# Attention sinks as one more score column, and the last query products and a stored group taken back one unit earlier

## The chip, the cores and the metric

The kernel runs on one core of one Trainium2 chip. The core has five engines that work side by side, each through a queue of its own in order: TensorE (PE in the profile, its weight loads PEld), VectorE (DVE), ScalarE (ACT), GpSimd (POOL), and SyncE (SP), which issues most of the transfers (DMA). The metric is the time of one execution on the device in microseconds, the median of several runs; lower is better.

## What is computed

A trunk of two layers with a batch of 1, 1024 positions and 1024 features in float32: an mLSTM mixer, a feed-forward part, a windowed attention mixer, another feed-forward part, with norms between them. The change touches only the attention. There 16 query heads share 4 key/value heads (4 query heads to a group), and every block of 128 queries sees the keys of its own block and of its two neighbours. Each query head has a *sink*, a number that takes part in the softmax as if it were one more key without a value:

```python
m = jnp.maximum(jnp.max(scores, axis=-1), sink_l)
p = jnp.exp(scores - m[..., None])
denom = jnp.sum(p, axis=-1) + jnp.exp(sink_l - m)
out = jnp.einsum('bchgqk,bckhd->bcqhgd', p, v_band)
out = out / denom.transpose(0, 1, 4, 2, 3)[..., None]
```

## The kernel before

The features lie on the partitions and the 1024 positions along the rows, in tiles of 128 x 1024 ("slabs") from one pool of 46. Each float32 product is made of three products of a high and a low part, and an operand is split by ACT (high part) and DVE or POOL (low part: source minus high part; helper `split`, line 203, and `split_scaled`, line 207; for weights line 190).

The attention (`attn`, line 1372) is one loop over 32 *units*, a unit being one group of four heads and one block of 128 queries, group by group: units 0 to 7 are group 0, 24 to 31 are group 3. Step `i` of the loop issues the softmax of unit `i` (`attn_soft`), the transposes of unit `i-2` (`attn_tr`, line 1313) and the products with the values of unit `i-3` (`attn_pv`, line 1328). Between them it places *fill*, products for TensorE that have nothing to do with the unit: until step 20 the query products of groups 1 to 3 (`rope_in`; a rotation on DVE and POOL, lines 1181 to 1191, ends each half, and line 1200 stores it in the DRAM tensor `bounce`), then the output products of groups 0 and 1 (`out_pair`). The numbers in `plan` say up to which step how many of the query pieces are placed.

The softmax of a unit (`head` and `scale`): TensorE makes the scores of a head with the sign turned (line 1284); one DVE instruction adds the mask, writes them to `e` and gives the smallest value, the negated sink included, to `mx` (`smm` in the trace, line 1289); ACT makes the exponential in place and sums it to `dn` (`smd`, line 1293), and makes the exponential of sink minus maximum in `ek` (`sme`, line 1294). For each pair of heads DVE adds `ek` to `dn` (line 1299) and takes the reciprocal (line 1300), and POOL multiplies the pair by it (line 1301). `e` has three buffers.

The outputs of groups 0 and 1 go to DRAM block by block (`ykeep`, line 1342) and come back as slabs: `take_back` issues the loads (line 724) and returns a function that splits them a step later. At step 20 (`NQ`) `load_x` issues 16 loads of the residual (line 242). At steps 6, 14 and 22 `load_q` and `load_k` load the next group's queries and keys (lines 1236, 1244). All these transfers stand in SP's one queue.

The Tile framework decides the order on each engine from the program's order, its priorities and its own estimate of times; the order is then fixed.

Of the kernel before, what the change touches and what calls it, by code (L numbers as in the profile page):

```python
# [11 lines left out]
F32 = mybir.dt.float32  # L12
F32R = mybir.dt.float32r
I32 = mybir.dt.int32
AF = mybir.ActivationFunctionType
ALU = mybir.AluOpType
# [3 lines left out]
P = 128  # L20
# [18 lines left out]
NQ = 20  # L39
# [15 lines left out]
def weave(main, fill=()):  # L55
    n = 0
    for i, m in enumerate(main):
        m()
        while n < len(fill) * (i + 1) // len(main):
            fill[n]()  # L60
            n += 1
# [20 lines left out]
class Trunk:  # L82
# [1185 lines left out]
    def attn_soft(self, g, b, st):  # L1268
        nc = self.nc
        V, A, G, T = nc.vector, nc.scalar, nc.gpsimd, nc.tensor  # L1270
        k0, nk = self.band(b)
        n = nk * P
        m0 = (k0 - (b - 1)) * P

        def head(hd):
            if hd == 0:
                st["e"] = self.t([P, 4, 3 * P], F32, "e", 3)
                st["m"] = [self.t([P, 4], F32, "sm" + x, 3) for x in "mde"]
            e, (mx, dn, ek) = st["e"], st["m"]
            qst, kk = self.qst[g], self.ks[g]  # L1280
            ps = self.bank("sc")
            lq = qst[hd // 2][:, (hd % 2) * S + b * P:(hd % 2) * S + (b + 1) * P]
            for j in range(2):
                T.matmul(  # L1284
                    ps[:, :n], lhsT=lq, rhs=kk[:, j * S + k0 * P:j * S + (k0 + nk) * P],
                    start=j == 0, stop=j == 1,
                )
            c, s = slice(hd, hd + 1), slice(4 * g + hd, 4 * g + hd + 1)
            V.tensor_tensor_reduce(  # L1289
                out=e[:, hd, :n], in0=ps[:, :n], in1=self.mask[:, m0:m0 + n], scale=1.0, scalar=self.nsink[:, s],  # L1290
                op0=ALU.add, op1=ALU.min, accum_out=mx[:, c],
            )
            A.activation(e[:, hd, :n], e[:, hd, :n], AF.Exp, bias=mx[:, c], scale=-1.0, accum_out=dn[:, c])  # L1293
            A.activation(ek[:, c], mx[:, c], AF.Exp, bias=self.sink[:, s])

        def scale(j):
            e, (mx, dn, ek) = st["e"], st["m"]
            d = dn[:, j:j + 2]
            V.tensor_tensor(d, d, ek[:, j:j + 2], op=ALU.add)  # L1299
            V.reciprocal(d, d)  # L1300
            G.tensor_tensor(  # L1301
                e[:, j:j + 2, :n], e[:, j:j + 2, :n], d.unsqueeze(2).broadcast_to([P, 2, n]), op=ALU.mult,
            )

        return [lambda hd=hd: head(hd) for hd in range(4)], [lambda j=j: scale(j) for j in (0, 2)]

    def attn_tr(self, g, b, st):
# [42 lines left out]
    def attn_setup(self):  # L1350
        nc = self.nc
        V, G = nc.vector, nc.gpsimd
        mask = self.mask = self.const.tile([P, 3 * P], F32, name="mask")
        G.memset(mask, 0.0)
        G.affine_select(
            out=mask[:, 0:P], in_=mask[:, 0:P], pattern=[[1, P]], compare_op=ALU.is_ge,
            fill=-NEG, base=0, channel_multiplier=-1,
        )
        G.affine_select(
            out=mask[:, 2 * P:], in_=mask[:, 2 * P:], pattern=[[-1, P]], compare_op=ALU.is_ge,  # L1360
            fill=-NEG, base=0, channel_multiplier=1,
        )
        raw = self.t([P, 16], F32, "sink", 1)
        nc.sync.dma_start(raw, self.h["sink"])
        self.sink, self.nsink = (self.const.tile([P, 16], F32, name=n) for n in ("sink", "nsink"))
        V.tensor_copy(self.sink, raw)
        V.tensor_scalar(self.nsink, raw, -1.0, None, op0=ALU.mult)

    def attn(self):
        nc = self.nc  # L1370

        def tables():
            for half in range(2):
                for tab in (self.cos, self.sin):
                    tb = tab[:, half * HALF:(half + 1) * HALF]
                    (nc.gpsimd if half else nc.vector).tensor_tensor(tb, tb, self.Rv(half), op=ALU.mult)

        with self.phase("a", 6, dict(mm=3, sc=2, tp=2, mx=1)):
            self.qst, self.ks, self.y23 = {}, {}, [[], []]
            weave(self.rope_in(1, -0.125, tables))  # L1380
            weave(self.rope_in(0, None))
            values = self.attn_values()
            values[4:4] = [lambda: self.load_q(0)]
            values[12:12] = [lambda: self.load_k(0)]
            weave(values)
            units = [(g, b) for g in range(4) for b in range(NC)]
            n = len(units)
            st = [{} for _ in units]
            qs = sum((self.rope_in(1 + g, -0.125) for g in range(1, 4)), [])
            y01 = [[], []]  # L1390
            outs = self.out_pair(y01)
            nq = len(qs) // 6
            for f in qs[:nq]:
                f()

            plan = ((0, nq), (4, len(qs) // 3), (11, 2 * len(qs) // 3), (21, len(qs)), (n + 3, len(qs)))
            no = 0
            backs = {}
            for i in range(n + 3):
                so, sc = self.attn_soft(*units[i], st[i]) if i < n else ([], [])  # L1400
                tr = self.attn_tr(*units[i - 2], st[i - 2]) if 2 <= i <= n + 1 else []
                pv = [lambda: self.attn_pv(*units[i - 3], st[i - 3])] if i >= 3 else []
                main = [pv, tr[:1], so[:1], tr[1:2], so[1:2], tr[2:], so[2:3] + sc[:1], so[3:], sc[1:]]
                main = [m for m in main if m]
                if i % NC == 6 and i < n - NC:
                    g = i // NC + 1
                    main[-1] += [lambda: self.load_q(g), lambda: self.load_k(g)]
                for j in range(2):
                    if i == (13, NQ)[j]:
                        backs[j] = self.take_back(self.ykeep[3 + j], y01[j])  # L1410
                    if i == (14, NQ + 1)[j]:
                        backs[j]()
                if i == NQ:
                    self.load_x(self.xkeep)
                (i0, n0), (i1, n1) = [(p, q) for p, q in zip(plan, plan[1:]) if p[0] <= i < q[0]][0]
                k = n0 + (n1 - n0) * (i + 1 - i0) // (i1 - i0)
                fill, nq = qs[nq:k], k
                if i > NQ:
                    k = len(outs) * (i - NQ) // (n + 2 - NQ)
                    fill, no = fill + outs[no:k], k  # L1420
                weave([lambda m=m: [f() for f in m] for m in main], fill)
            self.norm_begin(3, "forms")
            weave(self.out_pair(self.y23, True))
            self.norm_end()
# [98 lines left out]
```

## Time and profile before

| | |
|---|---|
| median of 3 runs | 2302.26 us (2301.77 to 2305.24) |
| the profiled execution, its own time | 2302.37 us |
| its span, first to last instruction | 2300.6 us |
| TensorE busy | 2216.2 us (96%) |
| VectorE busy | 1404.1 us (61%) |
| ScalarE busy | 837.9 us (36%) |
| GpSimd busy | 587.5 us (26%) |
| the attention's loop, units 0 to 31 | about 1285 to 1546 us of the span |

The profiled execution's time is 1.8 us more than its span, and 0.1 us above the median of the runs. "Busy" counts an instruction from start to end, so a stalled instruction is busy too, and TensorE's instructions overlap in its pipeline.

### The profile page before, as it was taken

What the parts mean: (1) busy time and instruction counts of PE and PEld (TensorE: products, weight loads), DVE (VectorE), ACT (ScalarE), POOL (GpSimd) and SP (SyncE); (2) the same over time, 40 slices, a digit from 0 to 9 for tenths busy, and PEclk for the clock granted to TensorE, in tenths of its full rate; (3) what the DMA queues carried; (4) which work ended last, traced back from release to release, by engine and by line L of the source; (5) the groups of instructions that cost most, each with busy time, mean ns of one, the idle gap of its engine ahead of it and who ended that gap; (6) DMA issues with size and microseconds to landing.
All of it is one profiled execution on the core that took longest, in us unless ns stands there. A gap on an engine that the chain in (4) does not pass through costs nothing.

```text
span 2300.6 us, 28252 instructions
## 1 busy us (share of the span) xinstructions
PE 2216.2 (96%) x10713; PEld 1822.1 (79%) x10713; DVE 1404.1 (61%) x2526; ACT 837.9 (36%) x1544; POOL 587.5 (26%) x398
## 2 busy tenths in 40 slices
PE   7899999998999999999999889898999999999998
PEld 4789888776888888878878777686888888888888
DVE  6455675688666666691224689778766666653112
ACT  4434444343222222321222578774422222232121
POOL 2212213311111111321343455550111111133143
PEclk9999999999999999999999999899999999999999
DMA  3111104232222222641322444602222222163112
GB/s 132 42 37 47 65 19 141 80 110 92 81 77 76 79 82 78 215 155 56 101 74 97 125 142 124 210 10 101 92 83 83 83 83 82 67 235 128 58 53 74
DMA packets 73655, 216.75 MB, mean 94 GB/s; under 512 B 8064, under 2 KB 14720, under 8 KB 73520
## 3 DMA queue, kind: packets, MB, share of 16 engines
q1 hardware_dynamic: 61912, 177.07, 23.5%
q10 hardware_dynamic: 11608, 37.89, 4.1%
q8 instruction: 84, 1.38, 0.2%
q14 instruction: 51, 0.42, 0.1%
HBM read 159.15 MB, written 55.77 MB: 93 GB/s over the span
## 4 chain that ended last, share of the span: by engine, by line
PE 43%; DVE 4%; DMA 3%; ACT 2%; POOL 2%; issue 1%; SPq 0%; POOLq 0%; ACTq 0%; DVEq 0%
PE mm L531 18%; PE mm L636 18%; PE mm L230 3%; DMA slab<-bounce 1%; DMA raw<-in_a_in_dram 1%; PE sc L1284 1%; PE mx L1328 1%; PE tp L1313 1%; ACT e L1293 1%; DMA slab<-ykeep 1%; DVE smd L1299 1%; DVE e L1289 1%; POOL slab L1191 0%; DVE t L203 0%; POOL e L1301 0%
## 5 line engine op out<-in xcount | busy, mean ns | idle before, releaser
L190 POOL TENSOR_TENSOR wl<-raw,wh 128x1024 fp32r<-128x1024 f32 (+2 forms) x96 | 228.7, 2386 | 602.6 <-ACT wh L189 379.2
L636 PE MATMUL mm<-hl,wh 128*128 128x512 f32 (+1 forms) x768 | 288.1, 375 | 1.3 <-DVE hl L611 1.3
L636 PE MATMUL mm<-hh,wl 128*128 128x512 f32 (+1 forms) x768 | 287.8, 375 | 0.1
L636 PE MATMUL mm<-hh,wh 128*128 128x512 f32 (+1 forms) x768 | 287.8, 376 | 0.0
L582 POOL TENSOR_TENSOR t<-t,R 128x512 f32<-128x512 f32 x44 | 58.2, 1322 | 595.1 <-ACT t L581 595.1
L663 DVE TENSOR_TENSOR x<-x,mm 128x512 f32<-128x512 f32 x80 | 54.6, 685 | 203.4 <-PE mm L636 203.4
L636 PEld LDWEIGHTS mm<-hl,wh 128*128 128x128 f32 x768 | 144.3, 188 | 30.0 <-DVE hl L611 1.7
L636 PEld LDWEIGHTS mm<-hh,wl 128*128 128x128 f32 x768 | 144.3, 188 | 28.8 <-POOL wl L190 0.5
L636 PEld LDWEIGHTS mm<-hh,wh 128*128 128x128 f32 x768 | 144.3, 188 | 28.2
L230 PE MATMUL mm<-slab,wh 128*128 128x512 f32 x512 | 152.9, 406 | 5.4 <-ACT wh L189 1.9
L581 ACT ACTIVATE t<-t 128x512 f32<-128x512 f32 x44 | 27.8, 632 | 327.5 <-DVE t L580 327.5
L531 PE MATMUL mm<-f12l,wbh 128*128 128x512 f32 x352 | 138.6, 394 | 0.0
L531 PE MATMUL mm<-f12h,wbl 128*128 128x512 f32 x352 | 138.4, 394 | 0.0
L531 PE MATMUL mm<-f12h,wbh 128*128 128x512 f32 x352 | 138.2, 394 | 0.0
L189 ACT ACTIVATE wh<-raw 128x1024 fp32r<-128x1024 f32 (+3 forms) x106 | 102.0, 968 | 68.4 <-DVE hl L611 43.5
L230 PE MATMUL mm<-hnh,wh 128*128 128x512 f32 x416 | 126.0, 402 | 0.9 <-DVE x L663 0.9
L573 DVE TENSOR_TENSOR t<-mm,t 128x512 f32<-128x512 f32 x44 | 30.4, 692 | 155.3 <-PE mm L531 155.3
L230 PE MATMUL mm<-hnh,wl 128*128 128x512 f32 x416 | 123.7, 398 | 0.4 <-POOL wl L190 0.4
L230 PE MATMUL mm<-hnl,wh 128*128 128x512 f32 x416 | 123.2, 397 | 0.0
L531 PE MATMUL mm<-f34h,wd 128*128 128x512 f32 x352 | 117.8, 395 | 0.0
L531 PE MATMUL mm<-f,wah 128*128 128x512 f32 x352 | 111.8, 398 | 5.7 <-DVE x L704 5.7
L230 PEld LDWEIGHTS mm<-slab,wh 128*128 128x128 f32 x512 | 95.3, 192 | 25.2 <-ACT wh L189 2.7
(291 smaller groups left out, 5285.5 us busy)
## 6 DMA issues: line engine op xcount, KB each, us to landing
raw<-in_ffn_in_dram SPq DMA_DIRECT2D x88, 512.0 KB
hkeep<-hs ACTq DMA_DIRECT2D x44, 512.0 KB
hraw<-hkeep SPq DMA_DIRECT2D x44, 512.0 KB
raw<-in_ffn_out_dram SPq DMA_DIRECT2D x32, 512.0 KB
raw<-in_m_in_dram SPq DMA_DIRECT2D x24, 512.0 KB
xkeep<-x ACTq DMA_DIRECT2D x24, 512.0 KB
bounce<-slab SPq DMA_DIRECT2D x40, 256.0 KB
x<-in_x_dram SPq DMA_DIRECT2D x32, 256.0 KB
```

The lines of the kernel that those rows point to most:

```text
L189: nc.scalar.activation(hi[:, c], r[:, c], AF.Copy)
L190: (nc.vector if fast else nc.gpsimd).tensor_tensor(lo[:, c], r[:, c], hi[:, c].bitcast(F32), op=ALU.subtract)
L230: self.nc.tensor.matmul(st["ps"], lhsT=l, rhs=r, start=j == 0, stop=j == len(jobs) - 1)
L531: self.nc.tensor.matmul(ps, lhsT=l, rhs=r, start=start and j == 0, stop=stop and j == len(jobs) - 1, skip_group_check=True,)
L573: V.tensor_tensor(u2, pb, p1, op=ALU.add)
L581: A.activation(g0, g0, AF.Silu)
L582: G.tensor_tensor(g0, g0, R0, op=ALU.mult)
L636: nc.tensor.matmul(po, lhsT=l, rhs=r, start=j == 0, stop=j == len(jobs) - 1)
L663: V.tensor_tensor(x, x, po, op=ALU.add)
L1284: T.matmul(ps[:, :n], lhsT=lq, rhs=kk[:, j * S + k0 * P:j * S + (k0 + nk) * P], start=j == 0, stop=j == 1,)
L1289: V.tensor_tensor_reduce(out=e[:, hd, :n], in0=ps[:, :n], in1=self.mask[:, m0:m0 + n], scale=1.0, scalar=self.nsink[:, s], op0=ALU.add, op ...
L1293: A.activation(e[:, hd, :n], e[:, hd, :n], AF.Exp, bias=mx[:, c], scale=-1.0, accum_out=dn[:, c])
```

## The change

The sink becomes one more column of `e`. At a unit's first head POOL copies the group's four negated sinks into column `n` of the four heads' rows (line 1279 of the changed kernel), and the exponential runs over `n + 1` columns, so that its sum holds the sink's term already. The separate exponential (`ek`, line 1294), DVE's addition (line 1299), the tile `sme` and the copy of the sinks in `attn_setup` go. The rows of `e` grow from 384 to 385 elements; POOL's scaling and the transposes still use `n` columns.

In `attn` the query products are all placed by step 19 instead of step 20, and the second stored group is loaded at step 19 and split at step 20, one step earlier each. `load_x` stays at step 20, and output products still start with step 21.

```diff
         def head(hd):
             if hd == 0:
-                st["e"] = self.t([P, 4, 3 * P], F32, "e", 3)
-                st["m"] = [self.t([P, 4], F32, "sm" + x, 3) for x in "mde"]
-            e, (mx, dn, ek) = st["e"], st["m"]
+                st["e"] = self.t([P, 4, 3 * P + 1], F32, "e", 3)
+                st["m"] = [self.t([P, 4], F32, "sm" + x, 3) for x in "md"]
+                G.tensor_copy(st["e"][:, :, n:n + 1], self.nsink[:, 4 * g:4 * g + 4].unsqueeze(2))
+            e, (mx, dn) = st["e"], st["m"]
...
-            A.activation(e[:, hd, :n], e[:, hd, :n], AF.Exp, bias=mx[:, c], scale=-1.0, accum_out=dn[:, c])
-            A.activation(ek[:, c], mx[:, c], AF.Exp, bias=self.sink[:, s])
+
+            x = e[:, hd, :n + 1]
+            A.activation(x, x, AF.Exp, bias=mx[:, c], scale=-1.0, accum_out=dn[:, c])
...
         def scale(j):
-            e, (mx, dn, ek) = st["e"], st["m"]
+            e, (mx, dn) = st["e"], st["m"]
             d = dn[:, j:j + 2]
-            V.tensor_tensor(d, d, ek[:, j:j + 2], op=ALU.add)
             V.reciprocal(d, d)
...
-        self.sink, self.nsink = (self.const.tile([P, 16], F32, name=n) for n in ("sink", "nsink"))
-        V.tensor_copy(self.sink, raw)
+        self.nsink = self.const.tile([P, 16], F32, name="nsink")
...
-            plan = ((0, nq), (4, len(qs) // 3), (11, 2 * len(qs) // 3), (21, len(qs)), (n + 3, len(qs)))
+            plan = ((0, nq), (4, len(qs) // 3), (11, 2 * len(qs) // 3), (20, len(qs)), (n + 3, len(qs)))
...
-                    if i == (13, NQ)[j]:
+                    if i == (13, NQ - 1)[j]:
                         backs[j] = self.take_back(self.ykeep[3 + j], y01[j])
-                    if i == (14, NQ + 1)[j]:
+                    if i == (14, NQ)[j]:
                         backs[j]()
```

Because the framework orders each queue anew, the change moves more than these lines. Two places are shown. The first is SP's queue around step 20, where `ykeep_67` is the store of group 1, `bounce_120` that of the last group's queries (each row with x2 stands for two stores) and `x_...` are the residual's loads. Before:

```order
L1342 DMA ykeep_67<-R_9190 256x1x128 x4
L1200 DMA bounce_120<-slab_12023 4x32x512
L170 DMA raw_12048<-in_a_out_dram 128x1024
L1200 DMA bounce_120<-slab_12023 4x32x512
L1200 DMA bounce_120<-slab_12024 4x32x512 x2
L724 DMA slab_12145<-ykeep_67 128x1024
L724 DMA slab_12146<-ykeep_67 128x1024
L242 DMA x_12149<-xkeep 128x512
...
L242 DMA x_12156<-xkeep 128x512
L1200 DMA bounce_120<-slab_12260 4x32x512 x2
L1200 DMA bounce_120<-slab_12261 4x32x512 x2
L1236 DMA slab_12456<-bounce_120 128x1024
```

and in the changed kernel:

```order
L1200 DMA bounce_120<-slab_11868 4x32x512 x2
L1200 DMA bounce_120<-slab_11869 4x32x512 x2
L170 DMA raw_11880<-in_a_out_dram 128x1024
L1343 DMA ykeep_67<-R_9188 256x1x128
L724 DMA slab_11954<-ykeep_67 128x1024
L724 DMA slab_11955<-ykeep_67 128x1024
L1200 DMA bounce_120<-slab_12041 4x32x512
L1200 DMA bounce_120<-slab_12042 4x32x512
L242 DMA x_12063<-xkeep 128x512
...
L242 DMA x_12070<-xkeep 128x512
L1236 DMA slab_12316<-bounce_120 128x1024
```

The last four of the eight stores of the last group's queries stood behind the 16 loads of the residual and stand ahead of them now; the loads of the stored group stand right behind the last store of that group and ahead of those four query stores.

The second place is POOL's queue in units 3 to 6. Before, where `e_10642`, `e_10741` and `e_10825` are the tiles of units 3, 4 and 5:

```order
L1301 TENSOR_TENSOR e_10642<-e_10642,smd_10644 128x768
L1190 TENSOR_TENSOR slab_10440<-slab_10440 128x512
L1191 TENSOR_TENSOR slab_10441<-slab_10441 128x512
L1301 TENSOR_TENSOR e_10642<-e_10642,smd_10644 128x768
L1301 TENSOR_TENSOR e_10741<-e_10741,smd_10743 128x768 x2
L1301 TENSOR_TENSOR e_10825<-e_10825,smd_10827 128x768 x2
L190 TENSOR_TENSOR wl_10894<-raw_10409,wh_10893 128x1024
```

and in the changed kernel, where `e_10622`, `e_10715`, `e_10793` and `e_10884` are those of units 3, 4, 5 and 6:

```order
L1302 TENSOR_TENSOR e_10622<-e_10622,smd_10624 128x2x384
L1190 TENSOR_TENSOR slab_10438<-slab_10438 128x512
L1191 TENSOR_TENSOR slab_10439<-slab_10439 128x512
L1302 TENSOR_TENSOR e_10622<-e_10622,smd_10624 128x2x384
L1279 COPY e_10793<-nsink 128x4
L1302 TENSOR_TENSOR e_10715<-e_10715,smd_10717 128x2x384 x2
L1279 COPY e_10884<-nsink 128x4
L1302 TENSOR_TENSOR e_10793<-e_10793,smd_10795 128x2x384 x2
```

The copy for unit 6 stands ahead of the scaling of unit 5; it has to wait until TensorE has transposed unit 3, which used the same buffer.

## Rows read from the trace of the kernel before

**Rows 1.** The page's busy time of each engine: us, share of the span, instructions.

```profile
PE 2216.2 (96%) x10713; PEld 1822.1 (79%) x10713; DVE 1404.1 (61%) x2526; ACT 837.9 (36%) x1544; POOL 587.5 (26%) x398
```

**Rows 2.** Stretches: length, busy PE, PEld, DVE, ACT, POOL, clock, DMA share, GB/s.

```profile
1285.00:1546.20 261.20, 236.56 (x1202) 191.48 (x1203) 220.15 (x585) 194.57 (x548) 145.04 (x105) 0.96 0.37 116
...
1285.60:1322.80 37.20, 31.80 (x156) 25.79 (x154) 31.90 (x79) 24.71 (x73) 19.19 (x14) 0.95 0.19 62
1322.80:1353.40 30.60, 29.87 (x167) 25.06 (x166) 26.23 (x77) 23.73 (x70) 15.24 (x11) 1.00 0.59 161
1353.40:1395.50 42.10, 35.78 (x178) 28.67 (x176) 38.05 (x90) 30.77 (x85) 23.57 (x16) 0.96 0.45 141
...
1431.80:1451.00 19.20, 13.93 (x67) 10.52 (x68) 16.73 (x41) 15.04 (x41) 15.41 (x12) 0.92 0.72 248
...
1465.80:1483.50 17.70, 14.01 (x70) 11.21 (x68) 8.33 (x26) 9.79 (x24) 7.40 (x7) 0.86 0.86 265
...
1479.70:1486.00 6.30, 6.26 (x22) 5.40 (x23) 1.87 (x8) 4.42 (x12) 3.51 (x3) 0.55 1.01 384
```

**Rows 3.** Groups by line and shape, 1285 to 1546: busy us, mean ns, idle before.

```profile
L1301 POOL TENSOR_TENSOR e<-e,smd 128x768 f32<-128x768 f32 x48 | 72.6, 1514 | 61.5 <-DVE smd L1300 48.3 <-ACT sme L1294 8.1 <-ACT t L202 2.2
...
L1293 ACT ACTIVATE e<-e,smm 128x384 f32<-128x384 f32 x96 | 58.5, 609 | 18.3 <-DVE smm L1289 17.2 <-DVE smd L1300 0.6
...
L1294 ACT ACTIVATE sme<-smm,sink 128x1 f32<-128x1 f32 x128 | 36.0, 281 | 0.0
...
L1299 DVE TENSOR_TENSOR smd<-smd,sme 128x2 f32<-128x2 f32 x64 | 29.7, 464 | 5.2 <-ACT sme L1294 5.0
...
L1301 POOL TENSOR_TENSOR e<-e,smd 128x512 f32<-128x512 f32 x16 | 16.6, 1040 | 39.7 <-ACT sme L1294 23.9 <-DVE smd L1300 14.2 <-ACT t L202 0.8
```

**Rows 4.** The chain that ended last, 1284 to 1547: shares; first, last ACT piece.

```profile
by line: PE mm L230 16.1%; DMA slab<-bounce 10.9%; PE sc L1284 7.5%; PE mx L1328 7.4%; PE tp L1313 7.3%; ACT e L1293 6.6%; DMA slab<-ykeep 5.2%; DVE smd L1299 4.9%; issue 4.6%; DVE e L1289 4.4%; DVE t L203 3.6%; POOL e L1301 3.3%; POOL slab
...
1302.82 0.19 ACT sme L1294
...
1527.83 0.19 ACT sme L1294
```

**Rows 5.** Timeline, 1296 to 1306, POOL and DVE: start us, us, instruction.

```profile
1296.88 1.74 POOL L1191 TENSOR_TENSOR slab<-slab 128x512 f32<-128x512 f32 x1
...
1297.39 0.15 DVE L1300 RECIPROCAL smd<-smd 128x2 f32<-128x2 f32 x1
...
1302.90 2.38 POOL L190 TENSOR_TENSOR wl<-raw,wh 128x1024 fp32r<-128x1024 f32 x1 [2.85 <-ACT wh L189]
...
1303.04 2.25 DVE L1299 TENSOR_TENSOR smd<-smd,sme 128x2 f32<-128x2 f32 x1 [0.18 <-ACT sme L1294]
```

**Rows 6.** Tile `smd`: shortest, median, longest ns; first and last start.

```profile
L1299 DVE TENSOR_TENSOR smd<-smd,sme x64: 132/164/2255, 1289.9 to 1534.7; 128x2 f32<-128x2 f32 x64
L1300 DVE RECIPROCAL smd<-smd x64: 145/160/167, 1290.8 to 1534.9; 128x2 f32<-128x2 f32 x64
```

**Rows 7.** SP's issues, timeline 1405 to 1490: start us, us, transfer.

```profile
1431.62 3.69 SPq L724 DMA_DIRECT2D slab<-ykeep  x2
1435.36 16.84 SPq L242 DMA_DIRECT2D x<-xkeep  x16
1452.58 3.83 SPq L1200 DMA_DIRECT2D bounce<-slab  x4
1467.40 2.27 SPq L1236 DMA_DIRECT2D slab<-bounce  x4
```

**Rows 8.** Timeline of PE: idle time before in brackets, and what ended it.

```profile
1448.25 1.65 PE L230 MATMUL mm<-slab,wh 128*128 128x512 f32 x3 [1.64 <-ACT slab L202]
...
1479.74 0.80 PE L1284 MATMUL sc<-slab,slab 128*128 128x256 f32 x2 [3.65 <-DMA slab<-bounce]
```

**Rows 9.** POOL by line and shape, whole span: the smallest instruction.

```profile
L1510 POOL MEMSET const-float32-1.0<- 128x1 f32 x1 | 0.1, 99 | 0.0
```

**Rows 10.** Who waited, 1285 to 1546: us in total, times, longest.

```profile
PE tp L1313 <- POOL e L1301: 3.1, 5, 1.5
```

## The prediction

> **What bounds the kernel now.** I read the page's busy times first [rows 1]: TensorE is busy for 96% of the span, so the rest of the kernel offers nothing to a change on other engines. The change lies in the attention's loop, so I read that stretch next. From 1285 to 1546.2 us TensorE has 236.6 us of busy time in 261.2, at a mean clock of 0.96 [rows 2]. Busy time hides what is lost, because overlapping or slowed matmuls count as busy; a better measure is how many matmuls pass. In the undisturbed stretch 1322.8 to 1353.4 there were 167 in 30.6 us, 0.183 us each, at full clock [rows 2]. At that rate the loop's 1202 matmuls would take 220 us, so about 41 us are lost to waits and low clock. The mix differs a little between stretches, so this is good to some us. The same count by stretch [rows 2] shows where:
>
> - 1285.6 to 1322.8: 156 matmuls, 28.6 us at that rate, 37.2 taken: 8.6 lost.
> - 1353.4 to 1395.5: 178, 32.6 us, 42.1 taken: 9.5 lost.
> - 1431.8 to 1451.0 (units 19 and 20): 67, 12.3 us, 19.2 taken: 6.9 lost.
> - 1465.8 to 1483.5 (the wait for group 3): 70, 12.8 us, 17.7 taken: 4.9 lost.
>
> The other 11 are spread over the rest. Then I asked what stands on the chain that ended last in the loop [rows 4]. VectorE's addition, line 1299, holds 4.9% of that 263 us window, 12.9 us, although it handles two numbers per partition. Its 64 instructions are busy for 29.7 us, a mean of 464 ns [rows 3], with a shortest of 132, a median of 164 and a longest of 2255 [rows 6]. The timeline tells why: the addition that started at 1303.04 ended at 1305.29, just after GpSimd's weight split from 1302.90 to 1305.28 [rows 5]. So it stands still until GpSimd is done, and what is queued behind it on VectorE (the next heads' mask and minimum, the low parts of the transposes) stands still too. The Trainium skill, SBUF — State Buffer, section "Who interferes with whom", gives a rule that agrees: a VectorE instruction with two inputs in SBUF blocks against a GpSimd instruction that reads SBUF. By that rule the addition's two inputs are what holds it.
>
> **What goes, what comes, what moves.**
>
> *The addition on VectorE goes.* Left as they were, 64 would cost their median 0.164 us, 10.5 us; the other 19 us are holds [rows 3, 6]. Of all this only the 12.9 us on the chain can shorten the loop [rows 4]; the lower end is zero, if the next late work is just as late, and the upper 12.9. The stretches that lose most (the first two above) are those where VectorE is nearly full, 31.9 us of 37.2 and 38.05 of 42.1 [rows 2], so there the removed time should come back. What is late next is the rotation of the query products on GpSimd, ScalarE and VectorE, with its own holds. I take 8.
>
> *The second exponential on ScalarE goes.* 128 instructions, 36.0 us busy, 281 ns each [rows 3]. ScalarE is at 194.6 us of 261.2 [rows 2], so most of this had slack. On the chain stand 30 pieces, the first at 1302.82 and the last at 1527.83, 0.19 us each [rows 4], about 5.5 us, two thirds of them behind 1395.5, where TensorE lost less to the softmax. Between 0 and 5.5 I take 1.5. The remaining exponential gets one column more: 609 ns for 384 [rows 3] is 1.6 ns a column, 0.2 us for all 128; nothing.
>
> *A copy on GpSimd comes*, 32 in all, three of them issued before the loop. The trace has no such copy. From below the nearest row is a write of one column, 99 ns [rows 9]; from above the smaller scaling, 1040 ns [rows 3]. Extrapolated from the two sizes of the scaling (512 elements 1040 ns, 768 elements 1514 ns: 1.85 ns an element) four elements cost some 0.1 us, so I take 0.1 to 0.2: 3 to 6 us on an engine with 145 us of 261 [rows 2]. It hides behind GpSimd's idle time, 101 us before the scalings alone [rows 3]. What matters more is its place: it stands ahead of the scaling of the unit before and waits for TensorE's transposes of three units earlier, and ScalarE's first exponential of its unit waits for it. Those transposes are done about one unit before that exponential, so cover is there; TensorE's own waits for the scaling were 3.1 us in the whole loop [rows 10]. I charge 0.5 us. With the upper end, 29 x 1.04, it would be 30 us on GpSimd, still under its idle time, with perhaps 5 on the path. The longer rows of `e` make the scaling two pieces instead of one run; the 512-element form, two pieces already, shows no extra price [rows 3].
>
> *The last query products move from steps 11 to 20 into steps 11 to 19*, so about a tenth more fill in each of them, the same 0.183 us per matmul. The gain is in SP's queue. Before, the last four query stores were issued at 1452.58, behind the 16 residual loads (1435.36, 16.84 us of issuing); the loads of group 3 had to wait for them and were issued at 1467.40 [rows 7]. Their queries came so late that TensorE idled 3.65 us before the first scores of unit 24 [rows 8] and then ran from 1479.7 to 1486.0 at a clock of 0.55, that is mostly at the lower level of 1.2 GHz [rows 2], which costs another 2.8 us. Now the stores stand ahead of the residual, and the loads of group 3 follow the residual's issues at once, some 10 us earlier. The four stores take 3.8 us to issue [rows 7]; the residual behind them comes that much later, with a unit or more of slack. Lost there: 4.9 us in the stretch, and 1 of the low clock after it. Between 0 and 5.9 I take 5.
>
> *The stored group comes back one step earlier.* Its two loads (issued at 1431.62, just ahead of the residual) now stand right behind the last store of that group and ahead of the four query stores; SP must wait for that store to land. Its splits still fall together with the rotation of the last query half, as before, since both moved by one unit; on the other hand the output products start a step after them instead of in the same step: before, TensorE idled 1.64 us at 1448.25 for such a split [rows 8]. Of the 6.9 us lost from 1431.8 to 1451.0 [rows 2] I take 3; from below −3, if step 20, which has no fill of its own now, leaves TensorE idle at a low clock.
>
> *The clock.* Fewer idle gaps mean fewer stretches below full clock: at 0.95 and 0.96 in the first two losing stretches [rows 2] some 3.5 us are lost to the clock alone, counted in the 8.6 and 9.5. I take 2 beside the 8.
>
> Sum: 8 + 1.5 − 0.5 + 5 + 3 + 2 = 19 us. The profiled execution took 2302.37 us, 1.8 more than its span and 0.1 above the median; 2302.3 − 19 = **2283 us**, 0.8% less.
>
> **Rivals.**
>
> 1. *The move gives nothing*: group 3 still waits, now for the residual's transfers, and units 19 and 20 pile up one unit earlier. For it: the 16 residual loads still stand ahead of group 3's loads. Then 19 − 8 = 11 us are left: 2291.
> 2. *The hold passes to the reciprocal.* VectorE's next instruction in line takes the addition's place and waits for GpSimd. Then the 8 shrinks to 1, and 12 us are left: 2290. Against it: none of the 64 reciprocals took more than 167 ns [rows 6], and one at 1297.39 ran its 0.15 us while GpSimd worked from 1296.88 to 1298.62 [rows 5]. But nearly all came right after an addition that had waited GpSimd out, so the test is thin. In the Trainium skill, on the same page and in the same section, a copy or a `tensor_scalar` with one input can take both ports and block against GpSimd too; the reciprocal is not named there. By that rule, if it held for the reciprocal, this rival is the case; the row at 1297.39 speaks against it.
> 3. *The whole loss goes*, because VectorE and ScalarE get slack of a unit and the new order holds together. Three quarters of 41 us are 30: 2272.
> 4. *No change*: what leaves the chain is replaced by work just as late. 2302.
> 5. *Slower: GpSimd's queue holds up ScalarE.* The copy sits behind a weight split (2.38 us [rows 5]) or the rotation, the first exponential waits, and so do scaling and transposes, unit after unit. The gain of 19 is used up at 0.6 us per unit over 32 units. At 0.8 us it would be 26 − 19 = 7 us slower: 2309. Against it: GpSimd idles for 116 us of the loop [rows 2], and a copy is early unless GpSimd is late by a unit.
>
> **How the numbers follow.** Forecast 0.48; rival 1 0.18; rival 2 0.06; rival 3 0.15; rival 4 0.08; rival 5 0.05. I take 0.2% (4.6 us) as what a measurement can tell from no change. Faster: 0.48 + 0.18 + 0.06 + 0.15 = 0.87; same 0.08; slower 0.05. The range leaves out rivals 4 and 5 and about a third of rival 3: 2272 to 2296, whose upper end is rival 1 with the addition's gain at half. The forecast's own range is 2277 to 2290.
>
> **What would show it.** VectorE's busy time in the loop falls by about 30 us, ScalarE's by 36; the reciprocal stays near 160 ns; copies of 0.1 to 0.2 us appear on GpSimd; TensorE's wait of 3.65 us for group 3 is gone, and no stretch near it runs at a clock of about half. The forecast is wrong if reciprocals of a microsecond appear, if ScalarE waits for the copy in many units, if TensorE waits longer at unit 20 for the stored group, or if the loop is no shorter though all these are as I say.

## The result and the profile after

The changed kernel takes 2290.39 us (median of 6 runs, 2288.08 to 2293.22), the kernel before 2303.00 us beside it (6 runs, 2301.77 to 2305.24): 0.9945 of the time, 95% interval 0.9932 to 0.9957. That is 12.6 us or 0.55% less. The forecast was 2283, so 6 of its 19 us are missing; the time lies inside the range and almost on rival 1's 2291. The profiled execution took 2290.14 us.

The page's busy times, which answer to [rows 1]:

```profile
PE 2213.5 (97%) x10713; PEld 1823.5 (80%) x10713; DVE 1378.8 (60%) x2461; ACT 816.9 (36%) x1416; POOL 592.5 (26%) x430
```

VectorE is busy for 25 us less and ScalarE for 21 (the prediction had about 30 and 36). The 36 us of small exponentials [rows 3] were a sum over instructions that overlap their neighbours (before, one ran from 1302.73 for 0.28 us, between instructions that ended at 1302.82 and started at 1302.91), so ScalarE gained only 21 of them. Groups by line and shape of the loop (1283 to 1535), which answer to [rows 3]:

```profile
L1302 POOL TENSOR_TENSOR e<-e,smd 128x768 f32<-128x768 f32 x48 | 71.7, 1498 | 34.8 <-DVE smd L1301 34.7
...
L1296 ACT ACTIVATE e<-e,smm 128x385 f32<-128x385 f32 x96 | 58.6, 612 | 17.3 <-DVE smm L1290 16.1 <-DVE smd L1301 0.3
...
L1279 POOL COPY e<-nsink 128x4 f32<-128x4 f32 x29 | 7.3, 251 | 17.9 <-PE tp L1314 17.8
```

and the tiles `smd` and `nsink` (shortest, median, longest ns), which answer to [rows 6]:

```profile
L1301 DVE RECIPROCAL smd<-smd x64: 152/160/168, 1291.6 to 1522.3; 128x2 f32<-128x2 f32 x64
```

```profile
L1279 POOL COPY e<-nsink x32: 189/192/654, 1202.9 to 1511.6; 128x4 f32<-128x4 f32 x32
```

The exponential of 385 columns takes 3 ns more than that of 384, the scaling of the longer rows nothing more, the copy 0.19 us in the median. GpSimd waits 17.8 us at the head of its queue with a copy, for TensorE's transposes, but ScalarE has no wait for a copy among its waits. The reciprocal, which has taken the addition's place on VectorE, is never held: rival 2 is out.

To see where time went I cut the loop at the first masked minimum of units 0, 14, 19 and 25 and counted matmuls as the prediction did (0.183 us each at full clock). Windows with the columns of [rows 2], first the kernel before:

```profile
1285.56:1395.54 109.98, 97.53 (x498) 79.52 (x496) 96.26 (x245) 79.25 (x227) 58.05 (x40) 0.97 0.40 120
1395.54:1431.83 36.29, 34.29 (x176) 26.15 (x176) 33.38 (x96) 30.28 (x87) 19.12 (x15) 1.00 0.35 92
1431.83:1487.50 55.67, 46.16 (x220) 36.94 (x221) 40.72 (x112) 39.03 (x110) 32.59 (x24) 0.88 0.69 236
```

then the changed kernel:

```profile
1287.38:1386.53 99.15, 92.68 (x499) 77.52 (x498) 80.53 (x218) 70.01 (x168) 60.66 (x52) 1.00 0.41 128
1386.53:1423.17 36.64, 32.74 (x167) 26.30 (x166) 29.51 (x82) 24.52 (x63) 19.59 (x19) 0.95 0.36 98
1423.17:1475.60 52.43, 45.06 (x230) 36.01 (x229) 39.36 (x107) 37.21 (x93) 33.23 (x32) 0.93 0.75 245
```

Length minus 0.183 us times the matmuls is what was lost: before 18.8, 4.1 and 15.4 us, 38.3 in all; after 7.8, 6.1 and 10.3, 24.2 in all. Units 0 to 13, where the move only adds a little fill (from step 11 on), gave 11.0 us. Units 14 to 24, where the move acts in full, gave 3.1.

The place of the move is SP's queue (timeline; start, us of issuing, transfer), to be read beside [rows 7]:

```profile
1421.96 0.77 SPq L1343 DMA_DIRECT2D ykeep<-R  x1
1432.35 0.80 SPq L724 DMA_DIRECT2D slab<-ykeep  x2
1433.25 6.17 SPq L1200 DMA_DIRECT2D bounce<-slab  x4
1439.47 15.52 SPq L242 DMA_DIRECT2D x<-xkeep  x16
1455.38 2.29 SPq L1236 DMA_DIRECT2D slab<-bounce  x4
```

The query stores do stand ahead of the residual, and group 3's loads were issued at 1455.38 instead of 1467.40. But unit 19 itself began at 1423.17 instead of 1431.83, so 8.7 of these 12 us are the faster units ahead of it. And between the group's last store, 1421.96, and its loads, 1432.35, SP stood still. Its waits, ScalarE's and TensorE's (timelines) name the reason:

```profile
SPq L724 <- DMA ykeep<-R: 9.7, 2, 9.5
```

```profile
1436.34 0.63 ACT L202 ACTIVATE slab<-slab 128x512 fp32r<-128x512 f32 x1 [4.60 <-DMA slab<-ykeep]
```

```profile
1437.02 2.16 PE L230 MATMUL mm<-slab,wh 128*128 128x512 f32 x4 [2.94 <-ACT slab L202]
```

SP waited 9.5 us for the store to land, ScalarE 4.60 for the loads behind it, TensorE 2.94 for the split; a window there and one just behind it show the clock fall to 0.75 and then 0.61, a mean of the two levels 1.2 and 2.4 GHz, in the second one mostly the lower:

```profile
1433.00:1439.40 6.40, 3.08 (x8) 1.96 (x9) 3.71 (x5) 2.65 (x5) 2.00 (x2) 0.75 0.59 195
```

```profile
1439.40:1444.00 4.60, 4.60 (x17) 3.84 (x17) 3.67 (x11) 2.87 (x8) 2.82 (x4) 0.61 0.69 251
```

And group 3 was still waited for, 2.6 us at the longest against 3.65 [rows 8]. The chain that ended last, from 1415 to 1480, consists almost only of transfers between 1421.96 and 1472.26 (start, us, what; short pieces left out):

```profile
1421.96 10.33 DMA ykeep<-R
...
1434.29 8.93 DMA bounce<-slab
...
1443.28 10.08 DMA x<-xkeep
...
1453.37 5.18 DMA x<-xkeep
...
1460.09 12.17 DMA slab<-bounce
```

### The profile page after: what moved, and what is told of

Same layout as the page of the kernel before. It is cut to its first block, busy times and chain, and to the rows that moved or that the text cites. A ratio compares the mean times of both kernels' runs of the same rounds, so it can differ in the third digit from the quotient of the medians.

```text
span 2288.4 us, 28098 instructions
## 1 busy us (share of the span) xinstructions
PE 2213.5 (97%) x10713; PEld 1823.5 (80%) x10713; DVE 1378.8 (60%) x2461; ACT 816.9 (36%) x1416; POOL 592.5 (26%) x430
## 4 chain that ended last, share of the span: by engine, by line
PE 46%; DMA 4%; DVE 3%; POOL 1%; issue 1%; ACT 1%; SPq 0%; POOLq 0%; DVEq 0%; ACTq 0%
PE mm L531 19%; PE mm L636 18%; PE mm L230 5%; PE sc L1285 1%; PE mx L1329 1%; DMA slab<-bounce 1%; PE tp L1314 1%; DMA raw<-in_a_in_dram 1%; DMA x<-xkeep 1%; DMA slab<-ykeep 1%; DMA ykeep<-R 0%; DMA bounce<-slab 0%; POOL slab L1191 0%; POOL slab L1190 0%; POOL e L1302 0%
```

## The experiments

Each kernel was timed in five rounds beside the kernel before, whose median was 2302.9 to 2303.6 us in these batches. "Lost" is worked out as above. One profile can differ from the median of its kernel by some 4 us.

### The two halves of the change

**The column alone**: the changed softmax, with `plan` and the steps of the stored group as before.

```diff
-... (20, len(qs)) ...   i == (13, NQ - 1)[j]   i == (14, NQ)[j]
+... (21, len(qs)) ...   i == (13, NQ)[j]       i == (14, NQ + 1)[j]
```

> Only the sink column; the last query products end at step 20 and the second stored group comes back at steps 20 and 21, as before the change. Against 2303 us before and 2290.4 us with the whole change. Theory A (the column alone gives the gain of the whole; the move's gain at the wait for group 3 is eaten by the new wait of 4.6 us for the stored group): 2288 to 2292, VectorE's line 1299 gone, no ScalarE wait for ykeep, the wait for group 3 still there. Theory B (the terms of the prediction: column 11, move 8): 2292 and a further gain from each part of the move.

Measured: 2292.05 us (2290.26 to 2296.31), 0.9946 [0.9934, 0.9958]: 11.1 us less than before. The windows of the same units:

```profile
1285.97:1387.21 101.24, 93.54 (x493) 77.59 (x493) 80.76 (x218) 69.59 (x168) 58.73 (x50) 0.98 0.41 120
1387.21:1422.30 35.09, 33.49 (x180) 26.79 (x180) 30.52 (x83) 27.36 (x69) 22.77 (x22) 1.00 0.40 114
1422.30:1476.79 54.49, 46.66 (x222) 37.21 (x222) 38.51 (x101) 35.40 (x87) 32.18 (x31) 0.87 0.73 248
```

Lost: 11.0, 2.2 and 13.9 us. The first differs by 3 us from the changed kernel's although the move only adds some fill there (499 matmuls against 493); most of it will be scatter between two profiles (the clock is 0.98 against 1.00). Behind it the move saves 3.6 us from unit 19 on and loses 3.9 in units 14 to 18, where 167 matmuls pass instead of 180 and the clock is 0.95 instead of 1.00. By the times the whole move is worth 1.7 us (2290.39 against 2292.05), and the two intervals are nearly the same: nothing that can be told from noise.

**The move alone**: the softmax of before with the new `plan` and steps (the same lines the other way round).

> The softmax as before (separate exponential, addition on VectorE), with the query products ending at step 19 and the stored group loaded at 19 and split at 20. Theory A: 2301 to 2306, the group 3 wait shorter but a wait of ScalarE for the stored group of 3 us or more. Theory B: 2295.

Measured: 2306.15 us (2303.98 to 2307.51), 1.0008 [1.0000, 1.0017]: nothing, or 3 us lost. SP waits 8.6 us for the store and ScalarE 3.3 for the loads, as in the changed kernel. The move isn't worth 8 with either softmax. Here unit 19 begins when it did before (1431.72 against 1431.83), so SP's queue can be read straight against [rows 7]:

```profile
1445.71 16.80 SPq L242 DMA_DIRECT2D x<-xkeep  x16
1462.86 2.31 SPq L1236 DMA_DIRECT2D slab<-bounce  x4
```

The residual is issued 10.4 us later, where the prediction took the 3.8 us of issuing the four stores, and group 3's loads 4.5 us earlier instead of some 10.

**The queries moved, the stored group not**, with the column:

```diff
-                    if i == (13, NQ - 1)[j]:
+                    if i == (13, NQ)[j]:
...
-                    if i == (14, NQ)[j]:
+                    if i == (14, NQ + 1)[j]:
```

> The column and the query products at step 19, but the stored group loaded at step 20 and split at step 21, as before. Theory A: the store of the group has landed by then, so the 4.6 us wait and the half clock behind it go and the earlier queries keep their gain: 2282 to 2287. Theory B: 3 us slower than the whole change, 2293.

Measured: 2291.56 us (2290.29 to 2292.75), 0.9941 [0.9929, 0.9953]; 0.5 us from the column alone. Theory A's 2282 to 2287 was missed: SP has no long wait for the group's store here, and the moved queries are still worth nothing. SP's queue of the column alone, which has the order of before:

```profile
1424.50 18.21 SPq L242 DMA_DIRECT2D x<-xkeep  x16
1458.31 1.75 SPq L1236 DMA_DIRECT2D slab<-bounce  x4
```

and of this kernel, with what SP waited for at the first of the four stores:

```profile
1434.59 3.81 SPq L1200 DMA_DIRECT2D bounce<-slab  x4
1440.99 16.23 SPq L242 DMA_DIRECT2D x<-xkeep  x16
1457.60 2.53 SPq L1236 DMA_DIRECT2D slab<-bounce  x4
```

```profile
SPq L1200 <- ACT slab L206: 17.8, 3, 10.4
```

Ahead of the residual the stores hold SP for 10.4 us, until ScalarE has split the last rotated queries; so the residual is issued 16 us later (2 of them because unit 19 begins later), and group 3's loads behind it only 0.7 us earlier.

**The stored group moved, the queries not**, with the column:

```diff
-... (20, len(qs)) ...
+... (21, len(qs)) ...
```

> The column and the stored group one step earlier, but the query products ending at step 20. Theory A: 2293 to 2297, as the wait for group 3 comes back; if the framework puts the stores ahead of the loads all the same, near the column alone. Theory B: 2289, the column plus 3.

Measured: 2288.00 us (2284.45 to 2290.7), 0.9923 [0.9911, 0.9936]; 4 us less than the column alone, though the two intervals touch. SP's queue has the same order in both, and ScalarE even waits 7.5 us for the group's loads in unit 20. The profile (of a run of 2289.58) does not show the gain in the loop: from the first to the last masked minimum it takes 236.4 us (1286.7 to 1523.1), the column alone 236.0. By medians this half is worth what the prediction took (3); that the move made it is not shown.

### What the column's 11 us consist of

**The addition without its hold**: the kernel before, its addition made by two instructions of one column, each with a pointer scalar.

```diff
-            V.tensor_tensor(d, d, ek[:, j:j + 2], op=ALU.add)
+            for c in (j, j + 1):
+                V.tensor_scalar(dn[:, c:c + 1], dn[:, c:c + 1], ek[:, c:c + 1], None, op0=ALU.add)
```

> The kernel before, with the addition of a pair (two tensor inputs in SBUF) made as two instructions with one tensor input and one per-partition scalar each; the second exponential on ScalarE stays. Theory H (the holds behind GpSimd are what the addition cost, and two tensor inputs are what is held): none of the 128 takes over 0.3 us, and the loop gains some 4 to 9 us of the column's 11: 2294 to 2299. Rival S (ScalarE's 128 exponentials were the cost): 2303, or some us more for the 64 extra instructions. Rival P (such an instruction is held as well): durations of a microsecond and more remain, 2303 or more.

Measured: 2298.17 us (2296.13 to 2304.51), 0.9981 [0.9972, 0.9990], 5.4 us less by the medians, 2.3 to 6.4 by the interval. The tile `smd`:

```profile
L1300 DVE TENSOR_SCALAR smd<-smd,sme x128: 190/207/216, 1288.6 to 1531.5; 128x1 f32<-128x1 f32 x128
```

Twice as many instructions, none above 216 ns where the addition went to 2255 [rows 6]. The Trainium skill, SBUF — State Buffer, "Who interferes with whom", has the blocked forms as those with two inputs in SBUF, and copies and `tensor_scalar` in their fast modes; the first agrees with the addition, and this `tensor_scalar` of one column was not held in 128 cases.

**The small exponentials kept**: the changed kernel, with ScalarE's 128 exponentials of one column put back and their results left unused.

```diff
+            A.activation(ek[:, c], self.nsink[:, s], AF.Exp, bias=mx[:, c], scale=-1.0)
```

> The changed kernel with ScalarE's 128 separate exponentials of one column put back; their result is not used, so VectorE has no addition and no wait for them. It tells what share of the column's 11 us was ScalarE's. Theory S (taking VectorE's addition without holds gave 5 us of the 11, and the other 6 are ScalarE's 36 us of small exponentials): 2294 to 2297 us, ScalarE's busy time in the loop up by about 36 us. Rival (they had slack; the whole 11 was VectorE's addition, its holds and its wait for the exponential): 2290 to 2292 us.

Measured: 2296.04 us (2294.16 to 2296.67), 0.9968 [0.9956, 0.9981], 5.7 us more than the changed kernel. ScalarE's busy time rises by 21 us to 837.6, not 36, as said above. The group by line:

```profile
L1297 ACT ACTIVATE sme<-nsink,smm 128x1 f32<-128x1 f32 x128 | 36.0, 282 | 0.0
```

and its window of units 0 to 13:

```profile
1287.43:1390.88 103.45, 95.60 (x495) 79.33 (x494) 80.40 (x217) 78.75 (x224) 59.44 (x51) 0.97 0.40 122
```

So they had little slack: 5.7 of the 11, where the prediction took 1.5. With the 5.4 of the addition the sum is 11.1, the column's whole gain, but that it meets so closely is luck. The masked minima, first and last start, give the length of the loop in each profile; in this order the kernel before, the addition without its hold, the column alone, the exponentials kept, and the changed kernel:

```profile
L1289 DVE CUSTOM_DVE_ANT_0 e<-sc,mask,nsink x128: 464/606/621, 1285.6 to 1532.6; 128x384 f32<-128x384 f32 x96, 128x256 f32<-128x256 f32 x32
L1289 DVE CUSTOM_DVE_ANT_0 e<-sc,mask,nsink x128: 462/606/620, 1284.4 to 1529.8; 128x384 f32<-128x384 f32 x96, 128x256 f32<-128x256 f32 x32
L1290 DVE CUSTOM_DVE_ANT_0 e<-sc,mask,nsink x128: 462/606/621, 1286.0 to 1522.0; 128x384 f32<-128x384 f32 x96, 128x256 f32<-128x256 f32 x32
L1290 DVE CUSTOM_DVE_ANT_0 e<-sc,mask,nsink x128: 462/608/623, 1287.4 to 1526.6; 128x384 f32<-128x384 f32 x96, 128x256 f32<-128x256 f32 x32
L1290 DVE CUSTOM_DVE_ANT_0 e<-sc,mask,nsink x128: 464/607/619, 1287.4 to 1520.7; 128x384 f32<-128x384 f32 x96, 128x256 f32<-128x256 f32 x32
```

That is 247.0, 245.4, 236.0, 239.2 and 233.3 us. The column's 11.0 and the exponentials' 5.9 are there in the loop, but of the addition's 5.4 only 1.6. So the holds are worth between 1.6 and 5.4, and up to 3.5 of the column's 11 has no run of its own; the additions themselves, which the two instructions of one column replaced and did not remove, and VectorE's wait for the exponential are left for it, but that is argued. Each edit also changes the order on TensorE (498, 503, 493, 495 and 499 matmuls pass in units 0 to 13), so a us or two of either share may be order.

**The copy on VectorE** instead of GpSimd.

```diff
-                G.tensor_copy(st["e"][:, :, n:n + 1], ...)
+                V.tensor_copy(st["e"][:, :, n:n + 1], ...)
```

> The whole change, but VectorE copies the negated sinks instead of GpSimd. Theory A (the copy on GpSimd lies in slack, its 17.8 us of waits for transposes included): within 3 us of the whole change's 2290. Rival Q (the copy holds up GpSimd's queue, and with it scalings and exponentials): 2283 to 2286.

Measured: 2288.08 us (2287.91 to 2292.76), 0.9943 [0.9930, 0.9955], no difference to the changed kernel. Yet the tile `nsink` shows it held:

```profile
L1279 DVE COPY e<-nsink x32: 149/172/1895, 1202.6 to 1514.0; 128x4 f32<-128x4 f32 x32
```

29 of them in the loop have a mean of 597 ns. One that started at 1303.00 ended at 1304.12, just after GpSimd's weight split of 1301.72 to 1304.10, as the addition did in [rows 5]. The same section of the Trainium skill names copies in their fast modes among what blocks against GpSimd; the trace agrees in so far as this copy was held. Here it cost nothing measurable. The length of a hold is not its price.

### Why the move gave so little

**Group 3's loads ahead of the residual**, both at step 20.

```diff
-                if i % NC == 6 and i < n - NC:
+                if i % NC == 6 and i < n - 2 * NC:
...
                 if i == NQ:
+                    self.load_q(3)
+                    self.load_k(3)
                     self.load_x(self.xkeep)
```

> The whole change, but the loads of group 3's queries and keys are issued at step 20 ahead of the 16 residual loads instead of at step 22 behind them. Theory V (in units 19 to 23 the transfers' volume sets the time: some 4 MB of residual stand in front of group 3's 3 MB): the wait for group 3 (2.6 us, and the short unit 23 of 12.7 us) goes, but the output products wait for the residual some 10 us later: 2286 to 2294, units 19 to 23 still about 49 us. Rival O (only the order matters, the volume fits): 2285 or less.

Measured: 2292.05 us (2290.92 to 2293.05), 0.9951 [0.9938, 0.9965]. Unit 23 falls to 10.3 us, but now VectorE waits 2.7 us for a row of the residual and TensorE 2.3 for VectorE. Which of the two goes first did not matter, as long as both were asked for at once.

**The residual spread**: its rows loaded two at a time at steps 20, 23, 26 and 29, in the order in which they are needed; the rest is the changed kernel.

```diff
-                if i == NQ:
-                    self.load_x(self.xkeep)
+                if i in (NQ, NQ + 3, NQ + 6, NQ + 9):
+                    self.x = [None] * KT if i == NQ else self.x
+                    for d in ((i - NQ) // 3, (i - NQ) // 3 + 4):
+                        self.x[d] = self.unit(name="x")
+                        for half in range(2):
+                            o = slice(half * HALF, (half + 1) * HALF)
+                            nc.sync.dma_start(self.x[d][:, o], self.xkeep[:, d, o])
```

> The whole change, but the residual's loads are spread: two feature rows each at steps 20, 23, 26 and 29 in the order in which the output products need them, so that 1 MB instead of 4 MB stands ahead of group 3's loads. Theory V: group 3's loads land 10 us earlier, nothing waits for them, units 20 to 23 lose 4 to 7 us less: 2283 to 2287. Rival K (units 19 and 20 lose their time to the stored group, and what is won at unit 23 was only waiting elsewhere): 2290.

Measured: 2284.69 us (2283.78 to 2285.4, 4 runs), 0.9920 [0.9906, 0.9933]: 5.7 us less than the changed kernel, the fastest of all. SP's timeline, and the windows of units 14 to 18 and 19 to 24:

```profile
1437.80 2.52 SPq L1419 DMA_DIRECT2D x<-xkeep  x4
1448.07 1.75 SPq L1236 DMA_DIRECT2D slab<-bounce  x4
```

```profile
1386.87:1421.70 34.83, 32.14 (x171) 25.61 (x170) 29.23 (x81) 24.00 (x61) 20.28 (x20) 1.00 0.40 115
1421.70:1470.73 49.03, 44.64 (x230) 36.03 (x229) 38.72 (x106) 36.92 (x94) 34.96 (x33) 0.93 0.70 236
```

Group 3's loads are issued at 1448.07 instead of 1455.38, TensorE's waits for them shrink to 1.2 us in all, and from unit 19 to 24 the same 230 matmuls as in the changed kernel pass in 49.03 us instead of 52.43. Units 23 and 24 take 12.2 us together instead of 15.5. The edit spreads the loads and puts them in another order at once (`load_x` loads the first halves of all rows ahead of the second); no run parts the two.

**The spread without the move** (`plan` and steps as before, the residual as just shown).

> The column alone, with neither the query products nor the stored group moved, and the residual's rows loaded two at a time at steps 20, 23, 26 and 29. Theory M (the move's gain was only masked by the residual's transfers; once they are spread, the moved queries and stored group are worth some us): slower than the spread version with the move (2284.7 us) by 2 to 4 us, 2287 to 2289 us. Rival (the move is worth nothing in either order of transfers): 2284 to 2286 us.

Measured: 2289.08 us (2287.43 to 2290.13), 0.9940 [0.9927, 0.9952]: 4.4 us above the spread with the move, and 3.0 below the column alone. Its TensorE waits 5.43 us for group 3, whose loads are issued at 1447.57, behind the residual's first four loads and the last query stores (timeline of PE; window of units 14 to 18):

```profile
1462.38 0.55 PE L1285 MATMUL sc<-slab,slab 128*128 128x256 f32 x1 [5.43 <-DMA slab<-bounce]
```

```profile
1385.18:1420.10 34.92, 33.33 (x179) 26.70 (x178) 30.52 (x83) 27.23 (x69) 22.60 (x22) 1.00 0.40 114
```

So the move has a worth of its own after all, 4.4 us against 1.7 without the spread. Group 3's loads are not issued earlier by it (1448.07 with the move); TensorE has more to do before it needs them, 230 matmuls in units 19 to 24 instead of 216. That the residual's transfers hid the difference fits these numbers but is argued: the profile here is of this kernel's fastest run, and in the two profiles the loop differs by 1.5 us only.

**The spread, and the stored group one step later** (load at step 20, split at 21, as before).

```diff
-                    if i == (13, NQ - 1)[j]:   ...   if i == (14, NQ)[j]:
+                    if i == (13, NQ)[j]:       ...   if i == (14, NQ + 1)[j]:
```

> The changed kernel with the residual's rows loaded two at a time at steps 20, 23, 26 and 29 (that alone gave 2284.7 us), and the stored group loaded at step 20 and split at step 21, as in the kernel before. Theory W (the store of the group has only just been issued when its loads are wanted; SP waits 9.5 us for it and ScalarE 4.6 us for the loads, and one step later the store has landed): unit 19 falls from 16 us to 11 to 13, ScalarE's wait for the stored group to below 2 us, and the time to 2279 to 2283 us. Rival (the transfers that are due there are the bound, so the stall goes to unit 20 or 21): units 19 to 23 together take what they took, 2284 to 2286 us.

Measured: 2291.56 us (2288.45 to 2294.7), 0.9953 [0.9939, 0.9967], 6.9 us more than the spread alone; neither theory had that. SP no longer waits for the store (0.2 us), and unit 19 does fall to 12.5 us, but unit 21 takes 14.1 for 33 matmuls. The loads now stand behind the last four query stores, ScalarE waits 5.79 us for them, and TensorE for ScalarE (timeline of PE):

```profile
1447.22 2.15 PE L230 MATMUL mm<-slab,wh 128*128 128x512 f32 x4 [5.45 <-ACT slab L202]
```

The step that looked like the fault, the early loads with SP's wait of 9.5 us, is the better place for them.

**The spread, with only the split a step later.**

```diff
-                    if i == (14, NQ)[j]:
+                    if i == (14, NQ + 1)[j]:
```

> The kernel with the spread residual (2284.7 us), the stored group loaded at step 19 as there, but split at step 21 instead of 20. Theory W (ScalarE stands at the head of its queue for the loaded group, 4.6 us, and the scores behind it on TensorE wait for its exponentials and splits): with a unit between load and split ScalarE does not wait, unit 19 falls to 12 us or less, 2280 to 2283 us. Rival (SP's queue behind the store is what counts): SP still waits 9.5 us, the time stays at 2284 to 2286 us.

Measured: 2286.17 us (2284.21 to 2287.24), 0.9927 [0.9914, 0.9939]: no gain over the spread. ScalarE's wait for the loads falls from 4.4 us to 0.7, and units 19 and 20 take 17.6 us instead of 23.7; but units 21 to 24 take 32.8 instead of 25.3, for 158 matmuls instead of 142, which account for 2.9 of the 7.5. SP still waits 9.5 for the store. Taking away the wait at the head of ScalarE's queue moved the loss on.

## Why the prediction was where it was

- **The column, 11 us in all (8 + 1.5 − 0.5 + 2): right in its sum**, 11.1 measured by itself, and in part by luck, for two terms were mis-sized and made up for each other. Removing the addition's holds is worth 1.6 (in the loop of the profiles) to 5.4 (by medians; 8, and part of the 2 for the clock, were taken), and the small exponentials 5.7 (1.5). The prediction set ScalarE's share low because ScalarE was busy for 194.6 us of 261.2 only, and because two thirds of its pieces on the chain lie behind 1395.5. But with the exponentials kept, units 0 to 13 lost 12.9 us (103.45 for 495 matmuls) instead of 7.8 (window above): the price seems to be paid mostly ahead of 1395.5 (up to 3 of these 5 us may be scatter, as the column alone lost 11.0 there), and neither the busy share nor a count of pieces on the chain told it. The copy's price and the reciprocal were as said.
- **The step that failed is "The last query products move", 5 us.** The stores do stand ahead of the residual, but the prediction priced them at the 3.8 us that it takes to issue them, "the residual behind them comes that much later", and not at SP's wait for their data. The residual came 10 us later with the softmax of before (1445.71 against 1435.36) and 15 to 16 later with the column (1439.47 and 1440.99 against 1424.50). So group 3's loads, which stand behind the residual in all these kernels, were issued 4.5, 2.9 and 0.7 us earlier, not some 10, and they *landed* no earlier. TensorE's first scores of unit 24, in the column alone and then in the changed kernel:

```profile
1469.89 0.79 PE L1285 MATMUL sc<-slab,slab 128*128 128x256 f32 x2 [4.84 <-DMA slab<-bounce]
1471.01 0.50 PE L1285 MATMUL sc<-slab,slab 128*128 128x256 f32 x2 [2.59 <-DMA slab<-bounce]
```

  The wait is shorter because TensorE comes to it later (at 1468.4 instead of 1465.0), not because the loads come sooner. The clock behind it did rise as the prediction hoped, from 0.61 (1469.89 to 1476.79, the column alone) to 1.00 (1472.40 to 1478.00). Store, residual and loads also share the transfer engines: the residual is 16 loads of 256 KB, 4 MB, and in the changed kernel's window just ahead of group 3's first scores the DMA share is 1.03 and the rate 273 GB/s, at which 4 MB are some 15 us (an estimate):

```profile
1460.10:1472.80 12.70, 9.92 (x57) 7.67 (x57) 8.61 (x23) 9.13 (x20) 5.98 (x8) 1.00 1.03 273
```

  This is rival 1 as it was written ("group 3 still waits, now for the residual's transfers"). The queries alone gave 0.5 us, and with the residual spread they made it 2.5 slower (2291.56 against 2289.08), and the 4.4 come out only when the group is moved as well.
- **"The stored group comes back one step earlier", 3 us: not confirmed.** By medians it gave 4 alone, without a trace in the loop of its profile, and 1.2 with the queries' move (2290.39 against 2291.56). The prediction saw that SP must wait for the store and set no price on it: 10.33 us on the chain, 4.60 on ScalarE, then a clock of 0.61. It named "TensorE waits longer at unit 20 for the stored group" as what would show it wrong; it came at unit 19, 2.94 us against 1.64.
- **What stays open.** Why the query products cost 3.9 us in units 14 to 18 with the residual in one piece and 1.3 with it spread (lost there 6.1 against 2.2, and 3.5 against 2.2): nothing of the residual is loaded yet in those units, the order and the clock (0.95 against 1.00) are left, and no run parts them. And of the 9.5 us that SP waits for the store, the runs don't tell what holds the store up; the transfer engines were not full, their share is 0.40 from 1421.96 to 1432.30.

## What to carry to other kernels

When a step is moved in a queue of transfers, price the landing and not the issue: ask first whether the data of what is moved ahead is ready, because everything behind it stands still until it is (10.4 us here). Then add up the bytes that are due in that stretch, and if they fill it, put off the ones that nobody needs yet (the residual, 5.7 us). Busy time and the length of a hold are poor prices on their own: 36 us of small exponentials with no idle time before them were worth 5.7 us, the holds in 30 us of additions 1.6 to 5.4, and 17 us of held copies nothing that could be measured. A wait at the head of a queue may be the cheapest place for it: both times that it was taken away from the spread kernel the loss came back in later units.

## What the runs showed of the hardware

- A VectorE copy of 4 columns with one input in SBUF took up to 1.9 us (median 0.17), and one of 1.12 us ended 0.02 us after a GpSimd instruction; reciprocals of 2 columns (64 of 64, at most 168 ns) and `tensor_scalar` of one column (128 of 128, at most 216 ns) were never held.
- A store of 128 KB (`ykeep`) took 10.33 us from issue to landing on the chain, as long as one of the residual's sixteen loads of 256 KB (10.08).
- GpSimd's copy of 4 columns costs 0.19 us, twice the MEMSET of [rows 9] and above what the two sizes of the scaling gave (0.1).
